# One fused two-block layer stack on one core: moved SBUF operands, a fixed tail for a recurrence, smaller blocks of a triangular inverse

## The chip, the core and the metric

The kernel runs on one core of a Trainium2 chip. The metric is the device time of one execution in microseconds (us), the median of several. The engines are TensorE (PE, with its weight loads listed as PEld), VectorE (DVE), ScalarE (ACT), GpSimd (POOL) and the queue engine SP, which issues the loads from HBM.

## What is computed

The input is 256 tokens of width 1024. Two layers of a first block come first. Each has a SwiGLU of width 2816, a mixer, and a second SwiGLU. The mixer has three branches (an RWKV-7 recurrence of six heads of 64, a dilated attention of six heads, a gated convolution of width 31), whose outputs are joined and multiplied by `w_out`. A second block of one layer follows, with a state-space branch, two attentions with 256 context tokens, gates, and a gated feed-forward with a convolution of width 3. The recurrence, which the change touches most, is

```
state = (state * w_t + (state @ a_t) * b_t + v_t * k_t)
y_t = state @ r_t
```

The reference scans it over the tokens. The kernel takes two chunks of 128 tokens. In each chunk the recurrence turns into products with the inverse of a unit triangular 128x128 matrix per head. The state `S1` goes from the first chunk to the second.

## The kernel before, in words

**Dense products.** Activations stand transposed, 128 features on the partitions and 256 tokens along the row. Weights come in chunks of eight 128x128 tiles (512 KB each) through three buffers `wraw`. ACT rounds a chunk to float32r (`whi`, L287), and DVE or POOL takes the rest (`wlo`, L263). Activations are split in the same way. A product of one weight tile is three float32r matmuls of 128x256: `whi` with the high part, `wlo` with the high part, `whi` with the low part (`dense`, L290 is the matmul of the helper `mm`). So each dense matmul loads its own 128x128 weights, while it streams 256 columns. In the page their outputs are named `gu` (gate and up), `dn` (down), `win` (the mixer's input projections), `woa` and `wob` (two parts of `w_out`), `c` and `p` (projections of the second block), `oa`, `ob`, `oc`, `o` (its outputs). The last `dn` has the activations as weights and streams 512 columns of weights.

**Where operands lie.** A pool lays tiles in SBUF in the order in which they are first asked for. In the built program all `whi` and `wlo` buffers start at 288 bytes modulo 512. The 18 activation tiles `xm` have rows of 258 floats, which are placed 1056 bytes apart, so that their starts run through all multiples of 32 modulo 512. The tiles `xr` and `mixr`, which feed `wob`, `oa` and `oc`, are 1024 bytes apart and all start at 480, which is 192 bytes behind the weights modulo 512. The big arenas `bigA` and `bigB`, which feed `dn`, start 64 bytes behind, and `F`, which feeds `c`, 352 bytes behind.

**The order of the work** is made by the tile framework's scheduler from the order of the code and from priorities (`first`). Instructions that are pinned (`pin`) keep the order of the program. Engines then run their lists in order and wait on semaphores.

**The recurrence** (`rwkv`, L683). `sc` are the products that fill, per head, four 128x128 blocks. `stream(0)` and `stream(1)` treat the two chunks, each with two groups of three heads. The inverse is built by doubling, in levels b = 2 to 64. For each level and group there are three matmuls `lt`, a mask by DVE (L263, `bigB<-lt,cb`), three matmuls `l`, an add by DVE (`bigA<-bigA,l`), and for b < 32 a transposition of 32x32 blocks by DVE (L787). Each of these float32 matmuls has 128x128 weights, streams 64 columns, and is done in two passes. Then come `z`, `u` (solve), `s` (state), `y` (output). The norm of `y` is the matmul `gv`, a chain of small DVE instructions for the reciprocal root, a copy over 384 columns (L912), and the matmul `gb`. DVE multiplies and adds, ACT and DVE split (`mixr`), and `wob` takes it. In `y` the three products of one head (with `U`, with `Vt`, with `S1`) follow each other, and the next head comes after them. The other branches and `woa`, which needs only the convolution and the attention, stand between these steps as the scheduler put them.

**The second block.** `qs` are matmuls that sum the squares of a query tile. They come right behind the projection whose squares ACT takes first. In the last feed-forward `gate_chunks` multiplies weight chunks of `cdown` by a gate, on DVE and POOL in turn, with three early chunks at n = 17, 19 and 21 of 22.

## Time and profile before

| | us |
|---|---|
| median of 3 runs | 1772.41 (1771.49 to 1832.52) |
| profiled execution, its own time | 1769.77 |
| its span, first to last instruction | 1767.9 |
| PE busy | 1718.1 (97%) |
| PEld busy | 1630.6 (92%) |
| DVE busy | 1371.7 (78%) |
| ACT busy | 942.1 (53%) |
| POOL busy | 519.4 (29%) |

A matmul of 128x256 takes about 280 ns from start to end, but the next begins long before that. What a dense stage costs is therefore the distance from one start to the next, which is read here as time divided by the count in a stretch (a stretch also counts the two or three that began up to 0.28 us ahead of it). Granted clock 1.00 is TensorE's upper level of 2.4 GHz, and a mean under 1.00 is a mixture with the lower one of 1.2 GHz.

### The profile page before, as it was taken

The numbers are of one execution on the slowest core, as the hardware profiler recorded it, in microseconds if no ns is written. First come the engines' busy times: TensorE is split into PE (matmuls) and PEld (weight loads), VectorE is DVE, ScalarE is ACT, GpSimd is POOL, SyncE is SP. The second block draws the span as 40 slices with busy tenths as digits, with TensorE's granted clock in tenths as the row PEclk, the third lists the DMA queues.
The fourth block names the chain that finished last, engine by engine and source line by source line (L and its number), as shares of the span: only waits on it lengthen the run. The fifth ranks groups of instructions, "written<-read, shape, count | busy, mean of one in ns | idle before, by whom it ended". The sixth has DMA issues, their size and how long they took to land.

```text
span 1767.9 us, 34289 instructions
## 1 busy us (share of the span) xinstructions
PE 1718.1 (97%) x13614; PEld 1630.6 (92%) x13614; DVE 1371.7 (78%) x2404; ACT 942.1 (53%) x1735; POOL 519.4 (29%) x457
## 2 busy tenths in 40 slices
PE   8999998989999999999998999999999999999998
PEld 8999996879999999999887999998988889999986
DVE  7885698748885778668885888968897776789888
ACT  5544476426444544447642544555666665466643
POOL 2221139222220022112942322024642131122143
PEclk9999999989999999999899999999999999999999
DMA  7665541015765577554101587554432225555533
GB/s 243 241 229 187 212 146 60 1 60 195 246 217 189 192 282 275 195 208 160 68 6 60 175 290 276 201 179 145 155 131 98 84 84 179 179 185 186 179 119 120
DMA packets 82128, 293.42 MB, mean 166 GB/s; under 512 B 9008, under 2 KB 10800, under 8 KB 81968
## 3 DMA queue, kind: packets, MB, share of 16 engines
q1 hardware_dynamic: 81968, 291.24, 47.1%
q8 instruction: 106, 1.74, 0.4%
q14 instruction: 54, 0.44, 0.1%
HBM read 290.15 MB, written 1.05 MB: 165 GB/s over the span
## 4 chain that ended last, share of the span: by engine, by line
PE 81%; DVE 10%; ACT 3%; issue 2%; POOL 2%; DMA 1%; SPq 0%; ACTq 0%; POOLq 0%; DVEq 0%
PE gu L290 32%; PE dn L290 17%; PE p L290 7%; PE win L290 4%; DVE wlo L263 3%; PE o L290 2%; PE woa L290 2%; DVE E L282 1%; PE lt L290 1%; PE l L290 1%; PE ob L290 1%; ACT whi L287 1%; PE y L290 1%; DVE E L263 1%; POOL E L263 1%
## 5 line engine op out<-in xcount | busy, mean ns | idle before, releaser
L287 ACT ACTIVATE whi<-wraw 128x1024 fp32r<-128x1024 f32 (+2 forms) x485 | 495.0, 1025 | 510.8 <-issue 180.7
L263 DVE TENSOR_TENSOR wlo<-wraw,whi 128x1024 fp32r<-128x1024 f32 (+1 forms) x445 | 550.2, 1237 | 193.5 <-ACT whi L287 184.9
L290 PE MATMUL gu<-xm,whi 128*128 128x256 f32 (+1 forms) x3520 | 631.5, 282 | 5.1 <-ACT whi L287 4.0
L290 PEld LDWEIGHTS gu<-xm,whi 128*128 128x128 f32 x3520 | 544.4, 190 | 6.4 <-ACT whi L287 4.3
L290 PE MATMUL gu<-xm,wlo 128*128 128x256 f32 (+1 forms) x1760 | 495.3, 282 | 2.4 <-DVE wlo L263 2.4
L290 PEld LDWEIGHTS gu<-xm,wlo 128*128 128x128 f32 x1760 | 333.4, 190 | 3.6 <-DVE wlo L263 3.6
L263 POOL TENSOR_TENSOR bigB<-E,bigA 128x256 fp32r<-128x256 f32 x110 | 144.8, 1319 | 557.0 <-ACT bigA L287 531.6
L290 PE MATMUL dn<-bigB,whi 128*128 128x256 f32 x704 | 196.6, 280 | 0.0
L290 PE MATMUL dn<-bigA,wlo 128*128 128x256 f32 x704 | 196.2, 279 | 0.0
L290 PE MATMUL dn<-bigA,whi 128*128 128x256 f32 x704 | 196.0, 279 | 0.0
L290 PE MATMUL p<-xm,whi 128*128 128x256 f32 x912 | 179.4, 290 | 1.8 <-DVE bigB L282 1.8
L290 PEld LDWEIGHTS p<-xm,whi 128*128 128x128 f32 x912 | 145.2, 190 | 8.4 <-issue 7.1
L263 POOL TENSOR_TENSOR E<-E 128x256 f32<-128x256 f32 x130 | 111.7, 884 | 96.1 <-ACT E L287 94.7
L290 PE MATMUL win<-xm,whi 128*128 128x256 f32 x736 | 139.0, 287 | 0.0
L290 PEld LDWEIGHTS dn<-bigA,wlo 128*128 128x128 f32 x704 | 132.1, 188 | 0.0
L290 PEld LDWEIGHTS dn<-bigB,whi 128*128 128x128 f32 x704 | 132.1, 188 | 0.0
L290 PEld LDWEIGHTS dn<-bigA,whi 128*128 128x128 f32 x704 | 131.6, 187 | 0.0
L290 PE MATMUL p<-xm,wlo 128*128 128x256 f32 x456 | 130.6, 286 | 0.0
L290 PEld LDWEIGHTS win<-xm,whi 128*128 128x128 f32 x736 | 114.9, 190 | 5.6 <-issue 5.6
L290 PE MATMUL win<-xm,wlo 128*128 128x256 f32 x368 | 104.0, 284 | 0.0
L263 POOL TENSOR_TENSOR wlo<-wraw,whi 128x512 fp32r<-128x512 f32 (+1 forms) x40 | 60.9, 1541 | 145.2 <-ACT whi L287 140.4
L263 DVE TENSOR_TENSOR E<-gu,rb 128x512 f32<-128x512 f32 (+1 forms) x136 | 78.3, 585 | 28.5 <-PE gu L290 28.3
(471 smaller groups left out, 3053.0 us busy)
## 6 DMA issues: line engine op xcount, KB each, us to landing
wraw<-in_wflat_dram SPq DMA_DIRECT2D x464, 512.0 KB, 3.5
E<-in_wmod_dram SPq DMA_DIRECT2D x48, 512.0 KB, 4.8
F<-in_wflat_dram SPq DMA_DIRECT2D x22, 512.0 KB, 4.3
E<-in_cc_dram SPq DMA_DIRECT2D x6, 512.0 KB, 5.9
cb<-in_cb_dram SPq DMA_DIRECT2D x2, 832.0 KB, 5.3
E<-in_ctxT_dram SPq DMA_DIRECT2D x1, 1024.0 KB, 6.1
out_dram<-E SPq DMA_DIRECT2D x4, 256.0 KB, 2.1
x<-in_xT_dram SPq DMA_DIRECT2D x3, 256.0 KB, 5.3
```

The costliest lines, as they stand in the source:

```text
L263: (eng or self.nc.vector).tensor_tensor(out=out, in0=a, in1=b, op=op)
L282: self.nc.vector.scalar_tensor_tensor(out=out, in0=a, scalar=s, in1=b, op0=op0, op1=op1)
L287: self.nc.scalar.activation(out=out, in_=a, func=func, **kw)
L290: return self.nc.tensor.matmul(out, l, r, start=start, stop=stop, skip_group_check=True)
```

## The change

1. **Addresses.** `xm` tiles lose two columns and so lie 1024 bytes apart. A dummy tile `gap` of 48 floats goes ahead of them, and `gap2` of 40 floats moves what comes later. The arena `E` is split in `Ea` and `Eb`. Tiles with 258 columns (the last feed-forward's input) and the input of `ob` move into `bigA` at strides of 384 and 256 floats. In the built program all moving operands of the dense products then start 192 bytes behind the weights modulo 512. In the last `dn`, where activations are the weights, they start 192 bytes behind the streamed operand.
2. **Ones products.** `turn` issues one extra 128x256 matmul with a matrix of ones as weights and an output that nobody reads, 26 in all.
3. **Quarter inverses.** The levels up to b = 32 work on the two 64x64 diagonal blocks apart (`halves`), six heads at a time. A final step of transposition and two products fills the upper right block.
4. **The tail** of the recurrence (`tail`) is pinned, with counted numbers of `woa` matmuls between its steps, and `y` goes through the heads once per kind of product.
5. **Moves.** The sums of squares of queries and keys (`q_end`, `mid`) come one projection later. `bkt` and `lo2` come behind the inverse. The early gated chunks come at n = 11, 13, 15, 17. `wlo` of `w_out` is taken by DVE instead of POOL. A multiplication by POOL in `ssm_core` is folded into DVE's add.

The core of the diff:

```diff
-    def xt(self, n=TOK):
-        return self.t([P, TOK + 2], "xm", bufs=XM, dt=F32R)[:, 0:n]
+    def xt(self):
+        return self.t([P, TOK], "xm", bufs=XM, dt=F32R)
...
+    def turn(self, x):
+        self.mm(self.pm("turn")[:, 0:TOK], self.ones_r, x, True, True)
...
+        self.t([P, GAP], "gap")
         self.xs = [self.prep(k, g0[:, k:k + 1], False) for k in range(KD)]
...
+            if n in (1, 2, 4, 10):
+                self.turn(xs[n % KD][0])
...
+            if n in (0, 3):
+                self.turn(hs[n][0])
...
+        def fill(n, pin=True):
+            for ins in itertools.islice(woa, n):
+                if pin:
+                    self.pin(ins)
+        fill(30, False)
+        tail(fill)
+        fill(200)
...
+            def twice(ps, u, w, x):
+                x2 = x.unsqueeze(1).to_broadcast([64, 2] + list(x.shape[1:]))
+                self.mm(ps[:, u * 32:u * 32 + 64], w, x2, True, True)
...
+            for b in (2, 4, 8, 16, 32):
+                ps = ring("lt")
+                for u in range(6):
+                    for h, o in enumerate(halves):
+                        twice(ps[o], u, N[o, c_ * 6 + u, h * 64:(h + 1) * 64], odd(MT[o, c_ * 6 + u, 0:64]))
+                self.mul(pv(Tm), pv(ps), lv)
+                ps = ring("l1")
+                for u in range(6):
+                    for o in halves:
+                        twice(ps[o], u, M[o, c_ * 6 + u, 0:64], Tm[o, u * 32:(u + 1) * 32])
+                self.add(mo, mo, pv(ps))
+                if b < 32:
+                    turned32()
...
+            copy_z(1)
+            fill(8)
+            u(1)
+            y1 = y(1)
+            rw0 = gv(0, sq0)
+            fill(4)
+            yc1, sq1 = y_end(1, y1, S1)
+            fill(13)
+            rw1 = gv(1, sq1)
+            gb(0, rw0, yc0)
+            fill(52)
+            gb(1, rw1, yc1)
...
+            if left:
+                q_end(*left)
             self.rope(tq, raw)
-            stack_q(i, tq)
+            left = i, sq, tq
...
-            if n >= NF - 5 and n % 2:
+            if n in (11, 13, 15, 17):
                 self.gate_chunks(self.ngated + 1)
```

On PE, in the tail of the first layer's recurrence, the list before reads as follows (`gv` and `gb` are the norm's two matmuls of the second chunk, `wob` is what consumes the result, L290 is the helper's matmul).

```order
L290 MATMUL y<-bigA,E 64x128
L290 MATMUL y<-bigB,S_3381 64x128
L290 MATMUL woa<-xm,wlo 128x256
L290 MATMUL woa<-xm,whi 128x256 x2
...
L290 MATMUL woa<-xm,wlo 128x256
L290 MATMUL woa<-xm,whi 128x256
L290 MATMUL gv<-cm,bigB 128x2 x3
L290 MATMUL gb<-cm,bigB 128x128 x3
L290 MATMUL wob<-mixr,whi 128x256
```

In the changed kernel the same place reads so (the helper's line is now L302; the first `gb` is the first chunk's, the second one the second chunk's).

```order
L302 MATMUL woa<-xm,wlo 128x256
L302 MATMUL gv<-cm,bigB 128x2 x3
L302 MATMUL gb<-cm,bigB 128x128 x3
L302 MATMUL woa<-xm,whi 128x256 x2
...
L302 MATMUL woa<-xm,whi 128x256
L302 MATMUL gb<-cm,bigB 128x128 x3
L302 MATMUL woa<-xm,whi 128x256
L302 MATMUL woa<-xm,wlo 128x256
...
L302 MATMUL woa<-xm,whi 128x256
L302 MATMUL wob<-mixr,whi 128x256
```

All `woa` matmuls stood ahead of the last `gv` before. Now 52 of them stand between the second chunk's `gv` and its `gb`, and 9 between `gb` and `wob`.

On PE, in the inverse of the first layer, the list before shows short groups of three per step, mixed with the attention (`apt`, `ao`, `asc`).

```order
L290 MATMUL lt<-bigA,bigB 128x64 x3
L290 MATMUL l_3505<-bigB 128x64 x3
L290 MATMUL l_3510<-bigB 128x64 x3
L294 MATMUL apt<-cm,F 128x128
L290 MATMUL ao<-F 64x256
L294 MATMUL apt<-cm,F 128x128 x2
```

In the changed kernel a step is twelve matmuls on 64 partitions of output each.

```order
L302 MATMUL lt<-bigA,bigB 64x64 x24
L302 MATMUL l_3218<-bigB 64x64 x12
L302 MATMUL l_3458<-bigB 64x64 x4
L306 MATMUL apt<-cm,F 128x128
L302 MATMUL l_3458<-bigB 64x64
L306 MATMUL apt<-cm,F 128x128 x2
```

The 24 `lt` are the first level of both chunks. The twelve of a chunk alternate between the upper left and the lower right quarter of the array.

## Rows read from the trace of the kernel before

**Rows 1.** The page: busy us, share of the span and instructions by engine.

```profile
PE 1718.1 (97%) x13614; PEld 1630.6 (92%) x13614; DVE 1371.7 (78%) x2404; ACT 942.1 (53%) x1735; POOL 519.4 (29%) x457
```

**Rows 2.** Waits of PE: us in total, times, longest.

```profile
PE gb L290 <- DVE bigB L912: 9.3, 2, 5.1
...
PE wob L290 <- ACT mixr L287: 3.2, 2, 1.6
...
PE qs L290 <- ACT kns L287: 2.6, 1, 2.6
```

**Rows 3.** Groups of matmuls on PE: count, busy us, mean ns, idle before.

```profile
L290 PE MATMUL gu<-xm,whi 128*128 128x256 f32 (+1 forms) x3520 | 631.5, 282 | 5.1 <-ACT whi L287 4.0 <-ACT xm L287 1.0
...
L290 PE MATMUL dn<-bigA,whi 128*128 128x256 f32 x704 | 196.0, 279 | 0.0
L290 PE MATMUL p<-xm,whi 128*128 128x256 f32 x912 | 179.4, 290 | 1.8 <-DVE bigB L282 1.8
L290 PE MATMUL win<-xm,whi 128*128 128x256 f32 x736 | 139.0, 287 | 0.0
...
L290 PE MATMUL lt<-bigA,bigB 128*128 128x64 f32 (+1 forms) x288 | 37.6, 268 | 3.4 <-DVE bigA L263 2.8 <-ACT E L287 0.4
```

**Rows 4.** Stretches: us, then busy (count) of each engine, PEclk, DMA, GB/s.

```profile
140.00:180.00 40.00, 40.00 (x342) 40.00 (x341) 22.32 (x28) 19.23 (x26) 4.12 (x5) 1.00 0.54 186
420.00:520.00 100.00, 100.00 (x850) 100.00 (x849) 81.62 (x109) 53.98 (x78) 25.16 (x19) 1.00 0.69 242
1626.00:1686.00 60.00, 60.00 (x501) 60.00 (x500) 53.61 (x97) 37.02 (x94) 9.90 (x10) 1.00 0.46 159
292.70:350.50 57.80, 54.02 (x413) 45.29 (x411) 46.89 (x142) 30.01 (x83) 27.95 (x32) 0.97 0.03 10
350.50:392.30 41.80, 35.14 (x285) 31.56 (x285) 18.07 (x51) 10.38 (x24) 12.86 (x10) 0.90 0.19 64
392.30:402.90 10.60, 10.60 (x72) 10.60 (x73) 5.70 (x13) 5.08 (x13) 2.06 (x3) 0.76 0.07 16
928.00:970.00 42.00, 36.10 (x296) 32.20 (x296) 21.62 (x58) 11.71 (x27) 12.50 (x10) 0.93 0.18 63
```

**Rows 5.** PE in order of time inside two runs of `oa`.

```profile
1503.97 0.28 PE L290 MATMUL oa<-xr,wlo 128*128 128x256 f32 x1
...
1505.03 0.28 PE L290 MATMUL oa<-xr,wlo 128*128 128x256 f32 x1
...
1511.76 0.28 PE L290 MATMUL oa<-xr,wlo 128*128 128x256 f32 x1
...
1513.12 0.28 PE L290 MATMUL oa<-xr,wlo 128*128 128x256 f32 x1
```

**Rows 6.** PE in order of time: small float32 matmuls of the recurrence.

```profile
319.93 0.83 PE L290 MATMUL lt<-bigA,bigB 128*128 128x64 f32 x6
...
342.66 0.56 PE L290 MATMUL l<-bigB 64*64 64x64 f32 x6
...
359.73 0.34 PE L290 MATMUL s<-bigB,E 128*64 128x64 f32 x4
...
360.48 0.28 PE L290 MATMUL y<-bigA,bigB 128*64 128x128 f32 x1
```

**Rows 7.** DVE on the tile `bigB`: duration ns min/median/max, first and last start us.

```profile
L787 DVE STREAM_TRANSPOSE bigB<-bigA x40: 546/566/579, 286.8 to 919.5; 128x384 f32<-128x384 f32 x40
L263 DVE TENSOR_TENSOR bigB<-lt,cb x40: 306/344/359, 295.7 to 921.4; 128x192 f32<-128x192 f32 x40
```

**Rows 8.** PE in order of time in the tail of the first layer.

```profile
375.76 0.43 PE L290 MATMUL y<-bigB,S 64*64 64x128 f32 x2
...
376.70 0.43 PE L290 MATMUL y<-bigB,S 64*64 64x128 f32 x2
...
389.07 1.62 PE L290 MATMUL gb<-cm,bigB 128*128 128x128 f32 x6 [5.08 <-DVE bigB L912]
392.27 0.58 PE L290 MATMUL wob<-mixr,whi 128*128 128x256 f32 x1 [1.58 <-ACT mixr L287]
```

More of the change, by code (lines that the diff above doesn't have):

```diff
@@ L1 @@
+import itertools
 import math
@@ L146, in _const_b1 @@
     parts = {}
-    for b in (1, 2, 4, 8, 16, 32, 64):
-        parts[f"lv{b}"] = (p // (2 * b) == f // (2 * b)) & (p % (2 * b) < b) & (f % (2 * b) >= b)
+    p2, f2 = p % 64, f[:, 0:64]
+    for b in (1, 2, 4, 8, 16, 32):
+        parts[f"lv{b}"] = (p2 // (2 * b) == f2 // (2 * b)) & (p2 % (2 * b) < b) & (f2 % (2 * b) >= b)
+    parts["id64"] = p2 == f2
     i = np.arange(TOK)[:, None]
@@ L331, in gate_chunks @@
             self.nc.sync.dma_start(out=r, in_=self.A["wflat"][off:off + P * w].rearrange("(p f) -> p f", p=P))
-            eng = self.nc.gpsimd if self.ngated % 2 else self.nc.vector
+            eng = self.nc.gpsimd if len(self.gated) < 4 and self.ngated - self.gate0 in (1, 3) else self.nc.vector
             self.pin(eng.tensor_tensor(out=r, in0=r, in1=self.g2, op=ALU.mult))
@@ L646, in mixer1, with products @@
         order_a = (6, 7, 3, 4, 5)
-        for n in range(KD):
-            ps = (self.pd, self.pm)[n % 2]("woa")
-            self.dense(ps[:, 0:TOK], [("w_out", l, k, n) for k in order_a], [self.mixh[k] for k in order_a])
-            self.add(self.x[n], ps[:, 0:TOK], self.x[n])
+        def products():
+            for n in range(KD):
+                ps = (self.pd, self.pm)[n % 2]("woa")
+                for i, k in enumerate(order_a):
+                    wh, wl = self.wtile(("w_out", l, k, n))
+                    xh, xl = self.mixh[k]
+                    for z, (w, x) in enumerate(((wh, xh), (wl, xh), (wh, xl))):
+                        ins = self.mm(ps[:, 0:TOK], w, x, i == z == 0, i == 4 and z == 2)
+                        if i == 4 and z == 2:
+                            self.add(self.x[n], ps[:, 0:TOK], self.x[n])
+                        yield ins
+        woa = products()
+        def fill(n, pin=True):
[5 more added lines that the diff above has]
+        fill(200)
         self.norm_begin()
@@ L814, in stream @@
                 for i in range(3):
-                    ps = ring("bon")
-                    self.mm(ps[:, 0:TOK], rkb[:, i, :], r[:, i, :], True, True)
-                    self.mul(bv[:, i, :], ps[:, 0:TOK], v[:, i, :])
-                for i in range(3):
                     ps = ring("lo2")
@@ L912, in stream @@
-            nc.vector.tensor_copy(rw, self.rsqrt(vv, 6, "r").unsqueeze(2).to_broadcast([P, 6, 64]))
-            rw = rw.rearrange("p (i h) d -> p i (h d)", h=2)
-            ps = ring("gb")
-            for i in range(3):
-                self.mm(ps[:, i * P:(i + 1) * P], rw[:, i], self.ident, True, True)
-            self.mul(yc, yc, v3(ps))
-            self.add(yc, yc, bv[:, :, ts_])
-            for i in range(3):
-                self.split(out[2 * i][:, ts_], out[2 * i + 1][:, ts_], yc[:, i])
+                copy_z(c_)
@@ L925, in rwkv @@
             self.mixh[i] = (out[2 * i], out[2 * i + 1])
+        return tail
     def conv(self, l, cb, col, cu, E):
@@ L1210, in ctx_path @@
                 self.act(hc[:, d, g * 512:(g + 1) * 512], ps)
-        end = self.knorm(kcc[:, TOK:512], proj(CK)[:, 0:TOK])
-        self.vtok(vcc, 2, proj(CV)[:, 0:TOK])
+        mid, end = self.knorm(kcc[:, TOK:512], proj(CK)[:, 0:TOK])
+        ps = proj(CV)
+        mid()
+        self.vtok(vcc, 2, ps[:, 0:TOK])
         end()
@@ L1237, in end @@
             self.stt(out, raw, self.gk, p3[:, 0:TOK], ALU.mult, ALU.mult)
-        return end
+        return mid, end
     def vtok(self, vcat, j0, ps):
@@ L1308, in block2, with q_end @@
         pss = self.pa("qs")
+        def q_end(i, sq, tq):
+            for tt in range(2):
+                self.mm(pss[:, i * 4 + 2 * tt:i * 4 + 2 * tt + 2], sq[:, tt * P:(tt + 1) * P], self.hsel, True, True)
+            stack_q(i, tq)
+        left = None
         for i in range(4):
@@ L1373, in block2 @@
             self.norm_add(v)
-            hi = self.xt()
-            lo = self.xt()
+            hi, lo = (yp[:, (2 * i + a) * TOK:(2 * i + a + 1) * TOK] for a in range(2))
             g = self.col("ssm_norm_2", i)
@@ L1412, in block2 @@
             self.stt(self.x[n], ps[:, 0:TOK], self.mod[:, 16 + n:17 + n], self.x[n])
-            xh, xl = self.xt(TOK + 2), self.xt(TOK + 2)
+            xh, xl = (gx[:, (2 * n + z) * XW:(2 * n + z) * XW + TOK + 2] for z in range(2))
             sh = self.mod[:, 24 + n:26 + n]
@@ L1654, in ffn_conv @@
             pr = pre[:, n % 3]
-            o = E(1024 + (n % 2) * 1024, TOK)
-            th = E(1024 + (n % 2) * 1024 + 256, TOK)
-            u = E(1024 + (n % 2) * 1024 + 512, TOK)
-            sc = E(3072 + (n % 2) * 4, 4)
+            o, th, u = (E(896 + (n % 2) * 768 + z * TOK, TOK) for z in range(3))
+            sc = E(2432 + (n % 2) * 4, 4)
             self.act(sc[:, 0:1], pg[:, TOK:TOK + 1])
```

284 lines of the change are left out of this document (156 added, 128 removed).

## The prediction

> **What bounds the kernel now.** I read the busy times first. PE is busy 97% of the span and PEld 92% [rows 1], so the question is at what rate PE works, and where it does not. Two further views answer it: PE's waits, which come to a few us at few places [rows 2], and the stretches, where a dense stage is read as time divided by matmuls [rows 4].
>
> In a `dn` stage 342 matmuls are counted in 40.00 us. One that began up to 0.28 us earlier is counted too, so the distance from start to start is 40.28/342 = 117.8 ns. In a `gu` stage it is 100.28/850 = 118.0 ns, and in the last feed-forward, with its 258 columns, 60.28/501 = 120.3 ns [rows 4]. Now look at `oa`, which has the same shape and the same three matmuls per weight tile. From 1511.76 to 1513.12 us there are 12 matmuls, 113.3 ns each. In a shorter run just before it there are 9 between 1503.97 and 1505.03, 117.8 ns each [rows 5]. The operands of `oa` start 192 bytes behind the weights in both runs. `dn` starts 64 bytes behind and never shows 113. So the trace has two steady rates, 113.3 and 117.8 ns, and the quick one stands in long runs only where the distance is 192 bytes, though not in every run there. DMA and DVE are busy in these stretches too, so they do not tell them apart.
>
> The rest of the time is in the recurrence. Its inverse fills most of 292.7 to 350.5 us, where PE is busy 54.0 of 57.8 us, and its tail 350.5 to 392.3, where PE is busy 35.1 of 41.8 us and the granted clock is 0.90 [rows 4].
>
> **The change part by part.** The sum is made against the profiled execution, 1769.8 us. The median of the runs shown is 2.6 us above it, which is added at the end.
>
> *Addresses.* The dense matmuls are 3520 and half as many for `gu`, three times 704 for `dn`, 912 and 736 with half as many again for `p` and `win` [rows 3], which is 9,864, and by the loops 984 more for `c`, `woa`, `ob` and `o`: 10,848. About 500 of them stand beside other work or at the lower clock, which leaves 10,300. Some 9,250 can go from 117.9 to 113.3 ns, 4.6 ns each, 42.5 us. Some 1,050 with 258 columns can go from 120.3 to 113.3 x 258/256 = 114.2, 6.4 us. The whole is 49 us. Not all runs at 192 bytes are quick. In rows 5 the long one is and the short one is not, and a long dense stage keeps whichever rate it fell into. The ones products put a matmul with another distance into each stage, which is a push out of a rate, and I take them to leave 80% of the time in the quick one: 39 us. The bounds are 20% and 100%, 10 and 49 us. The 26 extra matmuls cost 26 x 0.113 = 3 us. Net: -36 us.
>
> Are the weights there in time? A weight chunk is 24 matmuls, 2.83 us now and 2.72 us then. In `gu` DVE is busy 81.6 of 100 us [rows 4], which becomes 85, and in the last feed-forward 53.6 of 60, which becomes 94%. That cover is thin: if DVE were late there, that stage would keep up to 5 us of its gain.
>
> *Quarter inverses.* `lt` takes 288 passes [rows 3] and `l` as many. Six `lt` passes last 0.83 us, and one lasts 0.275, so they start (0.83 - 0.275)/5 = 0.111 us apart [rows 6]: 576 x 0.111 = 64 us for both layers. Then there are 1,056 passes with 64x64 weights (per chunk and layer five levels of 24 matmuls and a last step of 12, two passes each). Three rows bound their distance. Where two kinds of output halves alternate (`s`), 24 passes take 359.73 to 360.48, 31 ns each. On one and the same quarter (`l` 64*64) it is (0.56 - 0.27)/5 = 58 ns [rows 6]. Where tile shapes alternate, `y` needs 0.94 us for six passes, 157 ns each [rows 8]. The first two give 33 and 61 us. The new passes go back and forth between two quarters, as `s` does between two halves, so I take the value near `s`, 36 ns: 38 us, a gain of 26. DVE issues one mask, one add and one transposition for six heads instead of two of each.
>
> Is the path short enough to let PE have this? One level of a chunk is 24 passes (0.75 us) and their end (0.28), a mask of 0.34 [rows 7], again 0.75 and 0.28, an add of about the mask's length, and a transposition of 0.57 [rows 7], with the handing over about 3.8 us. Five levels are 19 us, and both chunks overlap. The attention fills the gaps. PE idles only 3.8 us in that stretch now [rows 4], so less work there is less time, until the convolution, which `woa` needs, becomes the late one. I keep 11 us per layer, -22 us, between 0 and -31.
>
> *The tail.* PE waits 9.3 us for the widened root and 3.2 us for the split of the result, over both layers [rows 2]. These are the 5.08 and 1.58 us of rows 8. In the new order `woa` stands behind both: 52 matmuls are 5.9 us, and 9 are 1.0 us. So the first wait goes, and part of the second stays. The lower clock goes with the idle time: a mean of 0.90 over 41.8 us, 0.76 over 10.6, 0.93 over 42.0 [rows 4] is 2 x (0.10 x 41.8 + 0.24 x 10.6 + 0.07 x 42.0) = 19 us at 1.2 GHz. The second layer's `wob` adds about what the first one's does, 5 us. Of these 24 us some 5 were idle, and the other 19 each lose half, 9.5 us. Together 22 us, of which I take 80%: -18 us, between -9 and -22. `y` of the second chunk goes through six heads per kind instead of changing the shape after every two passes. 36 passes at 157 ns [rows 8] are 5.7 us, and at some 80 ns (between 31 and 111 of rows 6) 2.9: -5 us for both layers, between 0 and -7.
>
> *The moves.* The wait of `qs`, 2.6 us [rows 2], goes, because a whole projection of 24 matmuls (2.7 us) now stands between the squares and the sums, and some time at the lower clock after it: -4 us, between -2 and -6. The steps late after that are the DVE ops of the rope, which were late before. The gated chunks, the folded multiplication and `wlo` of `w_out` on DVE move work to DVE where it is busy 18 of 42 us, or 80%: no change, at most 3 us either way.
>
> Sum: 36 + 22 + 18 + 5 + 4 = 85 us. 1769.8 - 85 = 1685, and 2.6 more on the median's scale: about 1687.
>
> **A rule that speaks against this.** Rows 5 show the same shapes at 113.3 and 117.8 ns, and rows 4 show 117.8 at another distance. The Trainium skill, SBUF — State Buffer, section "A bandwidth-pool intuition that's wrong (but worth ruling out)", says that TensorE has a second, independent read port for weight loads, and that what slows operations is a structural stall and not shared bandwidth. By that rule where the two operands lie would not matter; this case's trace does not agree, because its quick rate stands at one distance only, but it doesn't show the reason. The result that it would give is the first rival's.
>
> **The rivals.**
> *First: the dense rate does not change*, because the quick rate in `oa` comes from something else than the distance, or because each stage falls into 117.8 and stays. For it: the slow run of rows 5, at 192 bytes. Against it: `dn` in hundreds of matmuls never reaches 113. Without the 39 us the time is 1726, and with a fifth of the whole, 1716.
>
> *Second: the inverse gives nothing*, because its steps are a path through PE and DVE and not PE work, and the convolution on ACT and POOL is then the late one. For it: each step hands over three times. Against it: PE idles only 3.8 of 57.8 us. Time: 1687 + 22 = 1709.
>
> *Third, slower than before: changing the quarter of the array costs as much as changing the tile shape does in `y`.* Every second matmul of `lt` and `l` changes it. At 157 ns, 1,056 passes are 166 us instead of 64, 102 us more, while the other parts give 63: 1772.4 + 39 = 1811. The point from which it is slower is (64 + 63)/1056 = 120 ns per pass. For it: `y` in rows 8. Against it: `s`, which also alternates, at 31 ns.
>
> **How the numbers follow.** Forecast 0.60, first rival 0.20, second 0.15, third 0.05. A measurement can tell about 2% from no change: faster is under 1737, slower above 1808. The best ends of all parts (46 + 31 + 22 + 7 + 6 + 3 = 115 us) give 1657, and the low ends (7 + 0 + 9 + 0 + 2 - 3 = 15) 1757. Not all of these come together, so the range for 8 in 10 is 1655 to 1735, which takes in the first two rivals. The chances: faster 0.92 (forecast, second rival and nearly all of the first), within 2% 0.05, slower 0.03.
>
> **What would show it.** In the changed profile a `dn` stretch of 40 us would count about 355 matmuls at 113.3 ns, and 342 if the distance is worth nothing. The granted clock would be 1.00 through the tails, and the wait of `gb` for the widened root gone. `lt` passes would start 31 to 58 ns apart. From the first `lt` to the first `woa` it would be near 40 us instead of 58. The prediction is wrong if `dn` keeps 118 ns, if `lt` passes lie over 100 ns apart, or if PE waits in the last feed-forward for DVE.

## The result and the profile after

The changed kernel takes 1718.4 us (median of four runs, 1711.1 to 1727.4) where the kernel before takes 1772.4; the ratio is 0.970, with a 95% interval of 0.960 to 0.980. It is faster, and by less than forecast: 54 us instead of 85. Some executions of the kernel before and one each of two kernels below took over 1.5% longer than the fastest of the same kernel; the ratios, and all times below, leave them out. The four executions of the changed kernel fall into two pairs, 1711.1 and 1712.0 us with a mean granted clock of 0.987, and 1724.7 and 1727.4 with 0.979 and 0.978. The profiled one is of the longer pair. It took 1724.7 us, 45 less than the one of before, and its span is 1723.0.

The busy line of the page answers to [rows 1]:

```profile
PE 1670.9 (97%) x14120; PEld 1575.3 (91%) x14120; DVE 1345.4 (78%) x2381; ACT 945.1 (55%) x1735; POOL 450.0 (26%) x412
```

PE is still busy 97%, and its waits, which answer to [rows 2], have changed their places (us in total, times, longest):

```profile
PE apt L306 <- DVE F L288: 5.3, 8, 1.3
...
PE l L302 <- DVE bigB L275: 3.2, 4, 0.9
PE wob L302 <- ACT mixr L299: 3.0, 2, 1.5
PE gb L302 <- DVE bigB L974: 2.3, 2, 1.2
...
PE kn L302 <- ACT kns L299: 2.0, 1, 2.0
```

The wait of `gb` has fallen from 9.3 to 2.3 us, that of `wob` only from 3.2 to 3.0, and `qs` no longer appears. New are waits inside the inverse: `apt` (the transposed attention weights) and `l`, both for DVE, and a wait of the key sums `kn`.

The stretches of the changed kernel, with the columns of [rows 4]. The first three are a `dn` stage, a `gu` stage and the last feed-forward. Then each layer has two: from the first score product `sc` to the first variance sum `gv`, and from there to the next feed-forward:

```profile
140.00:180.00 40.00, 40.00 (x356) 40.00 (x355) 22.89 (x31) 19.70 (x26) 0.60 (x1) 1.00 0.60 189
420.00:520.00 100.00, 100.00 (x884) 100.00 (x884) 81.59 (x106) 49.76 (x74) 25.04 (x17) 1.00 0.71 232
...
1560.00:1620.00 60.00, 60.00 (x498) 60.00 (x498) 54.82 (x95) 36.99 (x92) 13.69 (x12) 1.00 0.55 178
...
260.00:358.70 98.70, 90.22 (x940) 70.61 (x940) 62.41 (x161) 50.92 (x123) 46.06 (x56) 0.90 0.10 32
358.70:383.60 24.90, 22.30 (x202) 21.41 (x200) 19.15 (x63) 10.22 (x24) 1.70 (x2) 1.00 0.27 86
812.90:927.70 114.80, 105.13 (x953) 81.86 (x953) 65.40 (x160) 51.68 (x124) 47.38 (x57) 0.79 0.10 29
927.70:952.60 24.90, 22.24 (x200) 21.37 (x199) 19.15 (x63) 10.21 (x24) 1.68 (x2) 1.00 0.28 86
```

The same four stretches of the recurrence in the kernel before:

```profile
267.80:365.80 98.00, 92.85 (x694) 78.15 (x694) 73.56 (x191) 49.73 (x123) 57.89 (x64) 0.98 0.11 37
365.80:402.90 37.10, 30.44 (x207) 27.78 (x207) 20.22 (x53) 11.11 (x27) 9.88 (x9) 0.82 0.15 47
845.90:942.00 96.10, 95.28 (x685) 80.82 (x685) 72.27 (x188) 49.89 (x122) 56.77 (x63) 0.93 0.08 28
942.00:980.30 38.30, 32.48 (x229) 29.74 (x228) 21.97 (x55) 12.21 (x29) 12.06 (x11) 0.87 0.22 74
```

Two things are to be seen. The dense stages have the quick rate: 40.28/356 = 113.1 ns in `dn` and 100.28/884 = 113.4 in `gu`, the last feed-forward has not (60.28/498 = 121.0). In the recurrence the part after `gv` fell from 37.1 and 38.3 to 24.9 us, with the clock at 1.00, 25.6 us less. But the part before it went from 98.0 to 98.7 us in one layer and from 96.1 to 114.8 in the other, 19.4 us more, and the granted clock there is now 0.90 and 0.79. The four stretches together gained 6.1 us, where the prediction's terms (22 + 18 + 5) had 45. That is the 39 us by which the profiled execution missed 1685.

How the 6.1 us divide cannot be read from the first `gv`, because the change moves it: in each layer 12 passes of `u`, 12 of `y` and two of `z` stood behind it before and stand ahead of it now. Two marks do not move, the first product of `win` and the next feed-forward. Between them lies the whole mixer; first the kernel before, then the changed one:

```profile
198.90:402.90 204.00, 191.01 (x1462) 171.80 (x1461) 153.97 (x347) 105.54 (x224) 92.45 (x94) 0.96 0.23 81
778.40:980.30 201.90, 194.07 (x1462) 175.04 (x1461) 152.29 (x340) 106.45 (x224) 90.48 (x94) 0.94 0.24 81
...
192.20:383.60 191.40, 178.93 (x1703) 156.62 (x1702) 142.55 (x327) 105.98 (x222) 71.31 (x79) 0.95 0.27 85
746.50:952.60 206.10, 192.20 (x1702) 166.22 (x1701) 141.48 (x320) 106.18 (x222) 71.69 (x79) 0.88 0.25 79
```

It took 405.9 us before in both layers together and takes 397.5 now.

### The profile page after: what moved, and what is told of

Same layout as the page of the kernel before. It is cut to its first block, busy times and chain, and to the rows that moved or that the text cites. A ratio compares the mean times of both kernels' runs of the same rounds, so it can differ in the third digit from the quotient of the medians.

```text
span 1723.0 us, 35217 instructions
## 1 busy us (share of the span) xinstructions
PE 1670.9 (97%) x14120; PEld 1575.3 (91%) x14120; DVE 1345.4 (78%) x2381; ACT 945.1 (55%) x1735; POOL 450.0 (26%) x412
## 4 chain that ended last, share of the span: by engine, by line
PE 83%; DVE 8%; POOL 4%; issue 2%; ACT 2%; DMA 0%; SPq 0%; POOLq 0%; DVEq 0%; ACTq 0%
PE gu L302 35%; PE dn L302 18%; PE p L302 7%; PE win L302 6%; PE o L302 2%; POOL Eb L275 2%; DVE wlo L275 2%; PE woa L302 1%; PE sc L302 1%; PE ob L302 1%; PE s L302 1%; PE y L302 1%; ACT whi L299 1%; DVE Eb L294 1%; PE pt L306 1%
## 5 line engine op out<-in xcount | busy, mean ns | idle before, releaser
L275 DVE TENSOR_TENSOR wlo<-wraw,whi 128x1024 fp32r<-128x1024 f32 (+2 forms) x477 | 573.7, 1203 | 169.2 <-ACT whi L299 166.0
L302 PE MATMUL gu<-xm,whi 128*128 128x256 f32 x2816 | 486.9, 278 | 6.5 <-ACT whi L299 3.8
L302 PEld LDWEIGHTS gu<-xm,whi 128*128 128x128 f32 x2816 | 428.2, 189 | 7.8 <-ACT whi L299 3.8
L302 PE MATMUL gu<-xm,wlo 128*128 128x256 f32 x1408 | 390.0, 278 | 2.2 <-DVE wlo L275 2.2
L302 PEld LDWEIGHTS gu<-xm,wlo 128*128 128x128 f32 x1408 | 265.4, 189 | 3.2 <-DVE wlo L275 3.1
L275 POOL TENSOR_TENSOR bigB<-Ea,bigA 128x256 fp32r<-128x256 f32 x88 | 122.7, 1397 | 420.3 <-ACT bigA L299 420.1
L302 PE MATMUL dn<-bigB,whi 128*128 128x256 f32 x704 | 194.1, 276 | 0.0
L302 PE MATMUL dn<-bigA,wlo 128*128 128x256 f32 x704 | 194.1, 276 | 0.0
L302 PE MATMUL dn<-bigA,whi 128*128 128x256 f32 x704 | 194.0, 276 | 0.0
L302 PE MATMUL p<-xm,whi 128*128 128x256 f32 x912 | 171.9, 285 | 0.7 <-DVE bigB L294 0.7
L302 PEld LDWEIGHTS p<-xm,whi 128*128 128x128 f32 x912 | 141.9, 188 | 6.9 <-issue 4.7
L302 PE MATMUL win<-xm,whi 128*128 128x256 f32 x736 | 139.5, 290 | 0.0
L302 PEld LDWEIGHTS dn<-bigA,wlo 128*128 128x128 f32 x704 | 132.1, 188 | 0.0
L302 PEld LDWEIGHTS dn<-bigB,whi 128*128 128x128 f32 x704 | 132.1, 188 | 0.0
L302 PEld LDWEIGHTS dn<-bigA,whi 128*128 128x128 f32 x704 | 132.0, 188 | 0.0
L275 POOL TENSOR_TENSOR Eb<-Eb 128x256 f32<-128x256 f32 x120 | 103.2, 886 | 104.3 <-ACT Eb L299 103.9
L302 PE MATMUL p<-xm,wlo 128*128 128x256 f32 x456 | 129.5, 284 | 0.0
L302 PE MATMUL gu<-bigA,whi 128*128 128x258 f32 x704 | 128.1, 284 | 0.0
L302 PEld LDWEIGHTS win<-xm,whi 128*128 128x128 f32 x736 | 117.2, 195 | 4.6 <-issue 4.6
L302 PEld LDWEIGHTS gu<-bigA,whi 128*128 128x128 f32 x704 | 109.9, 191 | 0.0
L302 PE MATMUL win<-xm,wlo 128*128 128x256 f32 x368 | 105.7, 288 | 0.0
```

Of the source, the lines that this page charges most:

```text
L275: (eng or self.nc.vector).tensor_tensor(out=out, in0=a, in1=b, op=op)
L302: return self.nc.tensor.matmul(out, l, r, start=start, stop=stop, skip_group_check=True)
```

## The experiments

Times are medians, with their range; ratios are to the kernel before. Every kernel is the changed one with the edit shown. "The stretch" is the one from the first `sc` to the first `gv`; the half clock is 1.2 GHz.

**The dense rate: distance or ones products.** First the distance alone (run b_dist64):

```
-GAP, GAP2 = 48, 40
+GAP, GAP2 = 16, 40
```

> The changed kernel with its gap one third as long, which puts most dense operands 64 bytes behind the weights instead of 192; ones products and recurrence stay. If the distance makes the quick rate: dn goes back to 117.8 ns and gu to 118, 2112 and 3 x 1056 matmuls and the projections, +35 to +45 us, 1746 to 1772. If the ones products make it at any distance: dn stays at 113.3 and the time at 1711 to 1727.

Measured: 1749.0 us (1747.9 to 1750.8), ratio 0.987 [0.982, 0.992]. The stretches of a `gu` stage, a `dn` stage and the last feed-forward:

```profile
20.00:120.00 100.00, 100.00 (x852) 100.00 (x851) 81.29 (x113) 50.09 (x74) 23.86 (x18) 1.00 0.72 236
145.00:185.00 40.00, 40.00 (x342) 40.00 (x342) 22.53 (x29) 18.48 (x24) 1.67 (x2) 1.00 0.58 184
1560.00:1620.00 60.00, 60.00 (x506) 60.00 (x506) 55.85 (x102) 39.28 (x99) 11.78 (x11) 1.00 0.58 182
```

`dn` counts 342 again, word for word what the kernel before counted, and `gu` 852: 117.8 and 117.7 ns, with all ones products in place. So it is where the operands lie. That it is the distance, and not the place of the moving operand by itself, is not separated: the weights start at 288 bytes modulo 512 in the kernel before, in the changed one and here. The last feed-forward, with its 258 columns, goes the other way: 506 matmuls, 119.1 ns at 64 bytes against 121.0 at 192.

Then the ones products, by leaving all 26 out (a_noturn):

```
-            if n in (1, 2, 4, 10):
-                self.turn(xs[n % KD][0])
...
-            if n in (0, 3):
-                self.turn(hs[n][0])
...
```

> The changed kernel without its 26 ones products; addresses and recurrence stay. If the ones products are what keeps the dense stages in the quick rate (113.3 ns per matmul), some of these stages fall back to 117.8 ns, as the short run of rows 5 did at 192 bytes: with half of some 10,000 dense matmuls at 4.5 ns more, minus 3 us for the products themselves, +15 to +20 us on the changed kernel's 1711 to 1727 us, so 1727 to 1747. If the distance of 192 bytes alone is enough, only their own time goes: 1708 to 1724, and dn keeps 113.3 ns.

Measured: 1716.6 us (1712.9 to 1719.9), ratio 0.969 [0.962, 0.977], as the changed kernel. Its first `gu` stage counts 885 in 100 us, and in its trace all eight stages with 256 columns run at 113 ns. That looked as if the ones products did nothing. A later run (n_fill) took them out once more, beside the fillers described below:

> The changed kernel with the 168 fillers in the score and inverse stages and without its 26 ones products in the dense stages. Theory: the dense stages keep 113.3 to 113.5 ns, the fillers keep the clock near 0.995, so it is the earlier run with both fillers less 3 us: 1702 to 1712, and the spread of its times is smaller than that of the changed kernel (16 us). Rival: the clock in the stretch is chance, and the times lie at 1711 to 1727 again.

Measured: 1719.1 us (1706.4 to 1727.7), ratio 0.968 [0.965, 0.972]. The clock was near 0.995 in all six runs, as expected, and still the times spread over 21 us. The stretches of the profiled run, 1727.7 us: the first `gu` stage, the first `dn` stage, and the third `gu` stage:

```profile
20.00:120.00 100.00, 100.00 (x851) 100.00 (x851) 82.66 (x114) 50.57 (x75) 25.30 (x18) 1.00 0.72 239
140.00:180.00 40.00, 40.00 (x342) 40.00 (x341) 22.33 (x28) 19.24 (x26) 4.07 (x4) 1.00 0.60 187
600.00:680.00 80.00, 80.00 (x708) 80.00 (x708) 66.84 (x87) 42.85 (x64) 24.64 (x17) 1.00 0.82 284
```

At one and the same distance the first two stages run at 117.8 ns and the third at 80.28/708 = 113.4. The third came in slow as well. What changed its rate is a product that the norm puts there, which has the same matrix of ones as weights (`nb`):

```profile
586.02 0.40 PE L302 MATMUL gu<-xm,whi 128*128 128x256 f32 x2
...
586.73 0.28 PE L302 MATMUL gu<-xm,whi 128*128 128x256 f32 x1
586.85 0.29 PE L302 MATMUL nb<-xm,ones 128*128 128x256 f32 x1
...
587.23 0.39 PE L302 MATMUL gu<-xm,whi 128*128 128x256 f32 x2
...
587.91 0.28 PE L302 MATMUL gu<-xm,whi 128*128 128x256 f32 x1
```

From 586.02 to 586.73 six matmuls start 118 ns apart, from 587.23 to 587.91 six start 113 ns apart. So 192 bytes make the quick rate possible, and a stage can keep the slow one for all its length. In this trace three of the four `gu` stages and two of the four `dn` stages are slow for nearly all their length: 4,224 matmuls at 4.4 ns more, an estimated 19 us. Less 3 us for the ones products left out, that is what this execution lies above the profiled one of the run with fillers and ones products (1727.7 against 1711.6). It can be why the theory failed although the clock was kept; the other five executions have no trace. The changed kernel's trace shows the push of an added product. PE in order of time around the first ones product of the last `gu` stage with 256 columns:

```profile
964.23 0.40 PE L302 MATMUL gu<-xm,whi 128*128 128x256 f32 x2
...
965.65 0.28 PE L302 MATMUL gu<-xm,whi 128*128 128x256 f32 x1
965.77 0.28 PE L302 MATMUL turn<-xm,ones 128*128 128x256 f32 x1
965.89 0.28 PE L302 MATMUL gu<-xm,whi 128*128 128x256 f32 x1
...
967.14 0.28 PE L302 MATMUL gu<-xm,whi 128*128 128x256 f32 x1
```

From 964.23 to 965.65 there are 12 matmuls, 118 ns each; from 965.89 to 967.14 there are 11, 114 ns each, and so it stays. In the traces of all runs at 192 bytes, 12 ones products in `gu` stand where the matmuls came in at the slow rate, and behind each of them the rate is the quick one; where it was quick already, in 333 places of `gu` and `dn`, it stayed so. At 64 bytes (b_dist64) none changed the rate. The quick rate can be lost too: in d_oldinv, a run described below, a `gu` stage falls to 118 ns behind a pause at 973.8 us, and the next ones product, at 1002.3, ends that.

Would more of them help the last feed-forward?

```
             self.pair((pg[:, 0:N2], pu[:, 0:N2]), ...
+            if n in (1, 2, 4, 10):
+                self.turn(xs[n % KD][0][:, 0:TOK])
...
-            if n == 0:
-                self.turn(ys[0][0])
+            if n in (0, 2, 4):
+                self.turn(ys[n][0])
```

> The changed kernel with six more ones products: after four weight rows of the last feed-forward and after the third and fifth row of ob. If the slow rate of these stages (120.8 ns for 258 columns, 117.8 ns in ob) is one they fell into, the push takes them to 114.2 and 113.3 ns: -7 and -1 us, 1704 to 1719. If it belongs to the 258 columns, 120.8 ns stays and only 0.7 us is added: 1711 to 1728.

Measured: 1714.8 us (1711.9 to 1718.2), ratio 0.968 [0.965, 0.971]. The last feed-forward counts 499 in 60 us: 120.8 ns. The slow rate belongs to the 258 columns at this distance.

**The recurrence, whole and in parts.** First the whole recurrence of the kernel before in the changed kernel (its functions and its masks are put back; c_oldrec):

```
-        tail = self.rwkv(l, cb, col, lt, ps_sh, R1, R2, E, conv_in, lambda: next(conv))
+        self.rwkv(l, cb, col, lt, ps_sh, R1, R2, E, conv_in, lambda: next(conv))
...
-        fill(30, False)
-        tail(fill)
-        fill(200)
+        ... eight dense groups of w_out, in a loop over n
```

> The changed kernel with the whole recurrence of the kernel before (full-height inverse, old order of the tail, no fillers); addresses, ones products and the moved steps of the last block stay. By the trace of the changed kernel the recurrence gave about 9 us in all (tails -26, the stretch from the first score product to the first variance sum +20, less what the addresses gave there): 1720 to 1738. By the prediction's terms (22 + 18 + 5) it gave 45 us: 1756 to 1772.

Measured: 1731.4 us (1731.2 to 1735.7), ratio 0.978 [0.971, 0.985]. The new recurrence is worth about 13 us, not 45, and what is not the recurrence about 41, near the forecast's 36 + 4. Then the old inverse with the new tail (d_oldinv):

```
-            for b in (2, 4, 8, 16, 32):
-                ... quarters, two heads per group side by side
+            for b in (2, 4, 8, 16, 32, 64):
+                ... full height, groups of three heads
```

> The changed kernel with the full-height inverse of the kernel before and the new tail. Theory: the quarter inverse saves PE 16 us of work per layer, but PE waits for DVE instead and the granted clock falls, so it gives nothing: here the stretch from the first score product to the first variance sum is 96 to 100 us in both layers with the clock mostly at 1.00, and the time is 1690 to 1718. Rival: the quarter inverse gives its 22 us and the loss is elsewhere in the stretch: 1733 to 1750.

Measured: 1712.3 us (1708.1 to 1712.8), ratio 0.966 [0.959, 0.973]. The stretch in both layers:

```profile
259.80:360.80 101.00, 96.10 (x700) 82.23 (x700) 73.45 (x197) 50.89 (x123) 46.04 (x54) 0.92 0.09 32
815.50:913.70 98.20, 96.74 (x713) 82.13 (x713) 74.11 (x196) 51.01 (x124) 46.61 (x55) 0.93 0.10 33
```

The theory holds, but for the clock, which is 0.92 and 0.93 and not mostly 1.00: with the full-height inverse the stretch is 101.0 and 98.2 us, and the kernel as fast as the changed one or a little faster. Everything that the recurrence gained comes from the tail. The whole mixer says the same; c_oldrec, then d_oldinv:

```profile
192.60:394.90 202.30, 192.37 (x1462) 172.99 (x1461) 158.13 (x364) 106.04 (x224) 72.63 (x78) 0.94 0.26 82
757.30:961.10 203.80, 195.40 (x1463) 175.51 (x1462) 152.31 (x357) 106.02 (x224) 72.35 (x78) 0.92 0.25 81
...
192.00:386.00 194.00, 185.04 (x1462) 168.48 (x1461) 152.90 (x363) 106.11 (x222) 72.48 (x77) 0.96 0.26 85
748.80:938.70 189.90, 184.24 (x1463) 166.72 (x1462) 151.71 (x356) 105.56 (x222) 70.54 (x77) 0.96 0.27 86
```

The new tail takes both layers from 406.1 to 383.9 us, 22 less; the medians differ by 19.

**What sets the length of the stretch.** If PE's work did, more of it would cost time. Ones products go in front of score and quarter products, into the tile that these then overwrite; in the second run in front of the score products alone:

```
                     ps = ring("sc")
+                    warm(2, ps)
...
                 ps = ring("lt")
+                warm(3, ps)
...
                 ps = ring("l1")
+                warm(3, ps)
```

> The changed kernel with ones products (128x256, float32r) in front of every score product pair (2 each, 24 per layer) and of every quarter product group of the five inverse levels (3 each, 60 per layer): 168 in all, 19 us at 113.3 ns if nothing hides them. Theory: the path through DVE, not PE, is the length of the stretch from the first score product to the first variance sum, and PE's waits lower its granted clock; then most of the 19 us falls into waits, the clock stays at 1.00 there (half-clock time under 10 us per layer against 20.5 and 47.8), the stretch is 88 to 100 us in both layers, and the time 1697 to 1717 us. Rival: PE's work sets the stretch, and the clock falls for another reason: +10 to +19 us, 1728 to 1745.

> The changed kernel with ones products in front of the score products alone (24 per layer, 5.4 us in all at full clock). Theory: the long stretch at 1.2 GHz that begins in the score products (27.3 us in the second layer of the profiled run) goes, and with it the two groups of times of the changed kernel (near 1711 and near 1726): 1705 to 1717. Rival: it makes no difference to the clock: +3 to +5 us, 1714 to 1731.

Measured: with both 1711.2 us (1705.9 to 1714.0); at the score products alone 1714.1 (1710.8 to 1722.9). The stretch with both:

```profile
260.20:360.40 100.20, 97.96 (x1036) 79.00 (x1035) 67.16 (x162) 51.34 (x123) 47.63 (x56) 0.97 0.10 33
814.70:913.30 98.60, 96.92 (x1038) 78.09 (x1038) 67.68 (x160) 51.89 (x124) 48.88 (x57) 1.00 0.11 34
```

19 us more of PE work cost nothing: the stretch is 100.2 and 98.6 us, the clock 0.97 and 1.00, and the 114.8 us of the second layer are gone. The fillers at the score products alone brought part of it. The whole mixer in the run with both:

```profile
192.80:385.30 192.50, 186.29 (x1786) 164.69 (x1785) 145.75 (x327) 106.56 (x222) 71.98 (x79) 0.97 0.27 84
748.30:938.50 190.20, 183.82 (x1787) 162.33 (x1786) 145.15 (x320) 106.71 (x222) 72.43 (x79) 1.00 0.28 85
```

That is 382.7 us for both layers, against 383.9 with the full-height inverse: with the clock kept, the quarter inverse is worth 1 us. So the stretch does not need all of PE's time, and even at full clock it is not shorter than before the change. The lower clock goes with the long second layer, but its mean alone does not make it: the run without ones products has 0.82 there, and 103.3 us.

Three runs leave out a part of what stands beside it:

```
# f_levels
-            for b in (2, 4, 8, 16, 32):
+            for b in (2, 32):
# g_attn
-        for i in range(3):
+        for i in range(1):
# g_taps
-        for j in range(31):
+        for j in range(8):
```

> The changed kernel with the levels 4, 8 and 16 of the inverse left out (that part of the computation is not done): per layer 288 of 528 quarter passes, 8 us of PE at 29 ns, and three rounds of product, mask, product, sum and transposition for each chunk. If the inverse's own path is the length of the stretch (about 4 to 8 us a level): 12 to 24 us per layer less, 1672 to 1695. If PE's work is: 8 us per layer, 1696 to 1710. If the attention beside it is the path: no change beyond 4 us, 1707 to 1726.

> The changed kernel with the windowed attention done for one pair of heads of three (the other two pairs are left out and take the first one's output): per layer PE work of 16 asc, 16 ao and 12 apt matmuls, about 8 us, and two rounds of scores, maxima, exponentials, sums and transpositions on DVE, ACT and POOL. If the attention is the path of the stretch: 15 to 25 us per layer less, 1670 to 1695. If PE's work is: 8 us per layer, 1696 to 1710. If the inverse's own path is: within 4 us, 1707 to 1726; the granted clock may fall further.

> The changed kernel with 8 of the 31 taps of the convolution (the other taps are left out): per layer 46 ACT scalings and 46 POOL additions of some 0.5 and 0.8 us less. Theory: the attention's biases on POOL and its steps on ACT stand behind the taps, so the path gets 6 to 14 us shorter per layer: 1686 to 1706. Rival: the convolution is hidden beside the rest: 1707 to 1727.

Measured: 1700.7 us (1693.0 to 1713.2) without three levels, 1686.2 (1682.0 to 1688.4) without two thirds of the attention, 1707.9 (1706.9 to 1715.6) without 23 taps. The stretch without the levels, then without the attention:

```profile
261.00:357.90 96.90, 90.29 (x653) 69.47 (x653) 56.42 (x143) 50.81 (x123) 45.95 (x56) 0.75 0.10 33
812.20:909.80 97.60, 89.89 (x665) 69.68 (x665) 57.94 (x142) 51.28 (x124) 47.57 (x57) 0.77 0.10 33
```

```profile
260.70:344.70 84.00, 75.74 (x897) 62.31 (x897) 54.20 (x133) 44.32 (x101) 37.36 (x48) 0.92 0.12 39
799.00:890.40 91.40, 83.76 (x910) 69.37 (x910) 56.60 (x132) 44.77 (x102) 38.66 (x49) 0.87 0.11 36
```

Three of five levels less, 288 matmuls less per layer, and the stretch is still 97 us: PE does less and gets a lower clock, 0.75 and 0.77. Without most of the attention it is 84.0 and 91.4 us, and the kernel 32 us faster, 16 per layer, where that part's PE work was put at 8. So the attention is on the path. The other two are less plain. By the medians the levels give 18 us, with a spread of 20 over four executions, which is in the range put down for PE's work, and the taps 10, at the edge of their rival's range. Against the run with fillers, where the clock was kept, the whole mixer is shorter by 3.5 us in both layers without the levels, by 5.2 without the taps and by 22.8 without the attention. Both the levels and the taps count little beside the attention, and these runs do not rank them. Nor was the rival tested that fewer levels would give more if the clock were kept: no run has fewer levels and fillers.

**Where it stands in the queues.** The trace of the changed kernel showed DVE held up by instructions that wait for ACT, 5.61 us each time, the first for the next layer's convolution weights:

```profile
305.17 0.20 DVE L288 TENSOR_SCALAR cwh<-cols 128x62 f32<-128x62 f32 x1 [5.61 <-ACT Eb L299]
...
883.49 0.42 DVE L275 TENSOR_TENSOR xm<-aof,xm 128x256 fp32r<-128x256 f32 x1 [5.61 <-ACT xm L299]
```

Both were taken away, alone and with the fillers:

```
-        self.ts(wh, col("conv_dw_w", 0, 62), 0.5, None)
+        self.pin(nc.vector.tensor_scalar(out=wh, in0=col("conv_dw_w", 0, 62), ...))
...
-            self.mix_out(3 + i, o)
+            self.mix_out(3 + i, o, gp)
```

> The changed kernel with two edits that take instructions out of DVE's queue which wait there for ACT: the next layer's convolution weights are kept in program order (in the trace of the changed kernel they held DVE up 5.6 us at 305 us, until the last tap was done), and the low part of the attention's three outputs is formed on POOL (on DVE they waited 1.5, 2.4, 2.7 and 5.6 us). Theory: DVE's blocked queue is part of the path, the stretch from the first score product to the first variance sum gets 5 to 10 us shorter in both layers and the granted clock falls less: 1690 to 1710. Rival: DVE has slack there: 1709 to 1727.

> The run before this one with the 168 ones products of the earlier run in front of the score products and of the quarter products. Theory: both gains add, since one shortens the path and the other keeps the clock: 1685 to 1705, clock at 0.993 or more. Rival: with a shorter path PE's work is the bound again, and 19 us of products cost 5 to 10 us against the run without them.

Measured: 1718.3 us (1711.8 to 1731.6) and 1719.2 (1713.4 to 1723.5). The rival was right in the first, theory and rival were both wrong in the second: these waits are not what the stretch hangs on.

Then the attention was moved as a whole, ahead of the score products by its projections, or behind the inverse by its priority:

```
# k_attnearly (m_earlyold: with the full-height inverse, l_earlyfill: with fillers)
             with self.first(PRI):
                 next(conv)
+            proj(14, len(order))
...
-        proj(14, len(order))
# k_attnlate
-        with self.first(1000):
-            self.attn1(l, cb, col, att, F)
+        self.attn1(l, cb, col, att, F)
```

> The changed kernel with the attention's nine projections placed ahead of the score products (before, they were filled in between them), so that the attention's steps begin some 20 us earlier and mostly stand ahead of the inverse. Theory: the stretch is long because the attention's and the inverse's dependent steps share DVE, ACT and POOL in one period; spread out, the time from the first projection to the end of the mixer falls by 8 to 16 us per layer from 191 to 206: 1690 to 1706. Rival: the work only moves, and the score products lose their cover: 1712 to 1735.

> The run before this one with the full-height inverse of the kernel before. Theory: where the attention is out of the way, PE's work counts again, and the quarter inverse gives its 16 us of PE work per layer in part: this run is 10 to 25 us slower than the one before it. Rival: the inverse's steps through DVE are the path anyway, and the two runs agree within 6 us.

Measured: 1742.7 us (1739.9 to 1744.0) with the quarter inverse and 1757.2 (1756.0 to 1758.0) with the full-height one. In both the projections are missing between the score products, and the clock falls (0.966 and 0.965 over the span), so this order is no gain; the first run lies above even its rival's range. But the pair answers what the quarter inverse is worth there. The stretch from the first `lt` to the first `gv` in both layers, first with quarters, then with full height:

```profile
326.70:373.10 46.40, 44.97 (x739) 38.74 (x738) 23.26 (x69) 15.59 (x36) 5.48 (x9) 0.96 0.05 14
902.60:944.60 42.00, 39.24 (x720) 35.01 (x719) 20.31 (x62) 11.47 (x26) 0.83 (x2) 1.00 0.05 15
```

```profile
319.50:382.70 63.20, 60.35 (x515) 54.59 (x513) 39.18 (x115) 20.72 (x51) 9.83 (x13) 0.95 0.03 9
899.70:959.00 59.30, 58.01 (x507) 53.33 (x506) 36.49 (x107) 16.02 (x39) 3.45 (x5) 0.94 0.03 10
```

With the attention mostly out of the way, this stretch is 17 us per layer shorter with quarters, and PE is busy 15 and 19 us less. But the first `lt` stands 37.3 and 38.0 us behind the first `sc` with quarters and 30.1 and 33.0 with full height. Over the whole mixer, 205.4 and 208.4 us against 215.0 and 213.2, the gain is 14.4 us in both layers, and that is the 14.5 us by which the times differ.

> The changed kernel without the raised priority of the attention, so that the steps of the inverse stand ahead of it where both are ready. Theory: the sum of both stays about the same, the inverse ends earlier and the attention's outputs, which the first output products need, later: within 6 us, 1708 to 1728. Rival: the attention's precedence was what held the inverse up: 1690 to 1706.

> The attention's projections first, as in the run above, and the 168 ones products in front of score and quarter products. Theory: with the clock at 0.99 or more and the steps spread out: 1685 to 1703, the lowest of all runs. Rival: PE's work counts again in the shorter stretch, and the products cost 8 to 19 us against the run without them.

> As the run above, with the attention's priority not raised. Theory: with the clock kept, the order of attention and inverse matters little, within 6 us of the run above, 1697 to 1712. Rival: the attention's outputs come late for the first output products and these fillers stand ahead of them: 1715 to 1730.

Measured: behind the inverse 1711.2 us (1703.4 to 1718.4); early with fillers 1780.4 (1779.1 to 1785.6); late with fillers and without the ones products 1742.9 (1727.6 to 1744.1). The first agrees with the theory that the order alone matters little. The other two were misses, as the early order without fillers was. Early, the fillers did not hold the clock: from 260 to 340 us it is 0.62 in that run. Late, the time lies above even the rival's range, and why was not followed further. None of these kernels beats the changed one by more than can be told: the lowest complete ones, 1711 us, have times that overlap with its 1711.1 to 1727.4.

## Why the prediction was right and wrong

*Addresses: right in mechanism and nearly in size.* The two rates, 113.3 and 117.8 ns, and their dependence on the distance are what b_dist64 shows, a difference of some 31 us by the medians. In the eight stages with 256 columns, 4,224 matmuls went from 118.0 to 113.4 ns and 2,112 from 117.8 to 113.1, 29 us. The ones products do what was assumed, a push out of the slow rate; how much they are worth depends on where a stage falls by itself, nothing that shows in a_noturn and some 19 us in n_fill's profiled execution. The Trainium skill, SBUF — State Buffer, section "A bandwidth-pool intuition that's wrong (but worth ruling out)", names a second, independent read port for weight loads; read as in the prediction, that would make the distance irrelevant, and the run that changes the distance alone does not agree with this reading, with 852 matmuls in 100 us against 884. The 6.4 us of the 258 columns were wrong: these do not have the quick rate at 192 bytes and lose 0.7 ns instead.

*The tail: right.* The waits of `gb` went from 9.3 to 2.3 us and the clock to 1.00. With the regrouped `y` the forecast was 18 + 5; between c_oldrec and d_oldinv, which differ by the tail, it is 22 us of the mixer and 19 of the medians. Part of the 25.6 us by which the part after `gv` is shorter is work that now stands ahead of it. Only the wait of `wob` stayed, 3.0 us.

*The quarter inverse: wrong, and with it the size of the whole.* Its passes are as quick as forecast:

```profile
315.99 0.91 PE L302 MATMUL l<-bigB 64*64 64x64 f32 x22
```

22 passes take 0.91 us and one 0.27, so they start 30 ns apart on average, where 36 was taken, and 58 and 111 before. The step that failed is "PE idles only 3.8 us in that stretch now, so less work there is less time". The term was -22 us; the quarter inverse gave 1 us with the clock kept, and cost 14 us of the mixer in the profiled execution (397.5 against 383.9). A PE that is busy 54.0 of 57.8 us [rows 4] was read as a PE that sets the time. It was busy, but the attention's steps through PE, DVE, ACT and POOL took just as long beside it, and when PE's share shrank, they stayed: that is the reading which the runs support best, since leaving the attention out is what shortens the mixer. This was the second rival's mechanism, with another late one: not mainly the convolution, which is worth 10 us by the medians when three quarters of it are left out, but the attention, worth 32. What was not foreseen at all is the way back through the clock: with the new waits PE is granted 0.90 and 0.79 of the clock, and the second layer is 16 us longer than in the run with fillers. That belongs to the longer pair of executions. In the shorter pair the gain is 61 us, and the 24 that are missing there are about the inverse's term.

The term was also a little too large in itself. The sum takes all 576 passes of `lt` and `l` at 111 ns. The 96 of the last level work on half or a quarter of the array and start 58 ns apart, as the row of `l` shows [rows 6], so PE's gain was nearer 21 us than 26.

The sign that was to show it misled, too. From the first `lt` to the first `woa` it is 41.2 us, near the 40 foretold. But in the new order the output products begin while the inverse still runs, as the chain of waits shows:

```profile
334.60 1.08 PE woa L302 x5
...
346.79 0.85 PE l L302 x12
```

The inverse ends at 347.6, 13 us after the first output product, and what counts is the stretch up to `gv`.

*The small terms.* The wait of `qs` went, and the key sums wait 2.0 us instead. The moved gating, counted as nothing, belongs to a last down stage that runs from 1650.0 to 1713.8 us, 63.8 instead of 68.8 before; this was not taken apart. The rival on the other side, a price of 157 ns per change of quarter, did not happen.

What stays open is which single step of the attention ends last, and whether it is its chain or its share of DVE, ACT and POOL that counts. Taking DVE's two longest waits away did not find it.

## What to carry to other kernels

A busy engine sets the time only if more work on it costs time: add some in the stretch before a large saving is counted on, and if that is free, look for the chain beside it, here by leaving out each neighbour in turn. Judge a stretch by marks that the change does not move: here the first `lt`, the first `woa` and the first `gv` all moved, and only the whole mixer agreed with the times. A stretch that is left with thin matmuls and waits can also lose the clock, and then the saving costs time.

## What the runs showed of the hardware

A dense float32r stage has two steady rates at one and the same distance of 192 bytes modulo 512, 113.4 and 117.8 ns per 256 columns, and can stay in either through the 100 us of a stage shown and on in the next; one product with another stationary operand (the matrix of ones) takes it from 118 to 114 ns, in 12 of 12 places, and a pause was seen to take it back. At 64 bytes only the slow one was seen with 256 columns, and with 258 columns 64 bytes are the better distance, 119.1 ns against 121.0.

Matmuls on two quarters of the array in turn start 30 ns apart on average, where on one quarter they need 58 ns.

PE can be busy 90.29 of 96.90 us by the profile and be granted 0.75 of the clock, with 653 matmuls, most of them small; with 1036 in nearly the same time, some 80 of them ones products, it was granted 0.97. Ones products did not always hold it: 0.62 from 260 to 340 us in the early order.
